# Expected durations of a hand-made instruction order reset, and its stream of weights rearranged

## The chip, the cores and the metric

The kernel runs on one core of a Trainium2 chip. The time is the device time of one execution in microseconds (us). A core has engines that run side by side, each taking its own queue of instructions strictly in order: TensorE (PE; PEld is its loading of weights), VectorE (DVE), ScalarE (ACT), GpSimd (POOL), and the queue of SyncE (SP), which here issues nearly all the transfers.

## The reference

One layer of a decoder trunk on 512 tokens of 1024 channels, in float32:

```
h = RMSNorm(x);  P = h @ W_in
y_A = attention: an indexer scores all keys, each query keeps its 128 best, softmax over those, 8 heads
y_B = HGRN2, a gated linear recurrence in chunks, 4 heads of 128, times silu(hg)
y_C = cb * causal_conv3(cc * ch)
x  += W_o( sum_b sigmoid(g_b) * (y_b @ U_b) )
x  += W_down relu(RMSNorm(x) @ W_up)^2
```

Columns of `W_in` are called kv (keys, values and the indexer's key), iq, aq (queries), hf, hq, hi, hg (HGRN2), cc, ch, cb (convolution) and g0, g1, g2 (the gates of attention, HGRN2 and convolution).

## The kernel before

**The stream.** All weights pass once, in 142 pieces ("slabs") of 128 rows times up to 1024 columns, in the order of `PLAN` (L32 to L47). For each slab SP loads `raw`, ACT rounds it to `whi` (fp32r), DVE forms `wlo = raw - whi` (L302 in `splitter`), and PE makes three products for each 128 x 128 block and 512 tokens (`whi` with the high and the low part of the other operand, `wlo` with the high part): 24 products of 512 columns for a full slab. Two `raw`, three `whi` and three `wlo` buffers stand between these steps. PE sums into tiles named `A` and the column's name (`Ahg`, `Ag`, `Au`, `Awo`, `Aup`, `Adn`).

**Beside the stream** run tasks. `index_task` chooses the best keys by 48 pairs of MAX and MATCH_REPLACE on DVE (L669, L670). `scan_task` takes each HGRN2 head through seven levels: an exponential on ACT (`Am`), a product on POOL (`Am` with `KQ`), two additions on DVE (`X`), products on PE (`pa`, or sums over channels `psum`, fed by a split `sh`, `sl`) and masked copies into `at` (L928, L945). `soft_task`, `soft_block`, `out_task` and `pv` do the attention of one head after another: logits (`pl`), softmax in `p`, transposes (`pt`), a split into `ph` and `pl`, products with the values (`po`), and `ya`; two heads make one of the four channel tiles of y_A. `pairs(b)` splits each finished channel tile of a branch into `yp`, which the raises `u` of that branch (`Au`) read. The raises of convolution (2), HGRN2 (1) and attention (0) follow in that order.

**What sets the order.** Class `Order` writes out the order of instructions of every engine when the program is built; the chip then only follows it. It keeps an expected clock for each engine. Every instruction has an expected duration `c` (L286 to L343), and a task's instruction is put on its engine's queue when what it reads is expected to be there. The stream goes first:

```
if e == "PE" and not main:
    at += self.SLACK                       # 250 ns
...
if not main and task.prio > 0 and e != "PE" and self.clk[e] > now + self.LIM:   # 900 ns
    self.push(self.clk[e] - self.LIM, task)
```

So a task's DVE, ACT or POOL work is put off while that engine is expected to be over 900 ns ahead of PE, and a task's product on PE is placed 250 ns after its operands are expected. The products of stream and tasks share PE's one queue: a task's product whose operand is late holds the stream behind it.

Of the kernel before, what the change touches and what calls it, by code (L numbers as in the profile page):

```python
# [21 lines left out]
EPS = 1e-6  # L22
# [9 lines left out]
def make_plan():  # L32
    plan = [("kv", 0)]
    plan += [("hf", j) for j in range(1, 4)] + [("hq", j) for j in range(4)] + [("hi", 0)]
    plan += [("hg", j) for j in range(4)] + [("aq", 0)]
    plan += [(c, j) for j in range(4) for c in ("cc", "ch", "cb")]
    for b in BRANCHES:
        for q in range(2):
            plan += [(f"g{b}", 4 * q + j) for j in range(4)] + [(f"u{b}", q)]
    plan += [("wo", j) for j in range(8)]  # L40
    for f in range(2):
        plan += [("up", 16 * f + j) for j in range(16)] + [("dn", 8 * f + j) for j in range(8)]
    return plan
# [6 lines left out]
def slabs_of(name, j):  # L50
    """The pieces of weights of one entry of the plan: matrix, first row, row blocks, first column, columns."""
    if name in FIRST_COL:
        return [("in", 0, 8, FIRST_COL[name] + 128 * j, 128)]
    if name == "kv":
        return [("kv", 0, 3, 0, 324), ("kv", 384, 3, 0, 324), ("kv", 768, 2, 0, 324)]
    if name in ("hi", "aq"):
        return [("in", 256 * i, 2, C_HI if name == "hi" else C_AQ, 512) for i in range(4)]
    if name[0] == "u" and name != "up":
        return [(name, 0, 4, 512 * j + 256 * i, 256) for i in range(2)]
    if name in ("wo", "up"):  # L60
        return [(name, 0, 8, 128 * j, 128)]
    return [("dn", 2048 * (j // 8) + 1024 * i, 8, 128 * (j % 8), 128) for i in range(2)]
# [34 lines left out]
class Order:  # L97
    """Fixes the order of instructions on each engine: the stream of weights runs through, and each of the tasks
    beside it goes on when what it reads is expected to be there."""

# [51 lines left out]
    def step(self, task, main=False):  # L152
        """Goes on with a task as far as it can now; for the main stream only one group of products at a time."""
        while True:
# [97 lines left out]
def kernel(ctx: ExitStack, tc: tile.TileContext, xT, x, wst, slabs, vecs, rel, ident_d, masks_d,  # L252
# [26 lines left out]

# [1 line left out]
    def in_psum(*aps):  # L281
# [4 lines left out]
    def act(out_, in_, func, scale=None, bias=None, accum=None):  # L286
        kw = {}
        c = 100 + 0.83 * size(in_)
        if scale is not None:
            kw["scale"] = scale  # L290
            c += 0 if isinstance(scale, float) else 93
        if bias is not None:
            kw["bias"] = bias
            c += 93
        if accum is not None:
            kw["accum_out"] = accum
            c += 90
        return Op("A", c, [in_, scale, bias], [out_, accum], lambda: A.activation(out_, in_, func, **kw))  # L298

    def tt(out_, a, b, op, e="V"):  # L300
        c = 65 + 1.06 * size(out_) if e == "V" else 110 + 2.2 * size(out_)
        return Op(e, c, [a, b], [out_], lambda: (V if e == "V" else G).tensor_tensor(out_, a, b, op))  # L302

    def ts(out_, a, s1, s2, op0, op1=None, e="V"):
        n = size(out_)
        c = (65 + (1.06 if in_psum(a) else 0.53) * n) if e == "V" else 100 + 1.0 * n
        eng = V if e == "V" else G
        f = (lambda: eng.tensor_scalar(out_, a, s1, s2, op0)) if op1 is None else (
            lambda: eng.tensor_scalar(out_, a, s1, s2, op0, op1))
        return Op(e, c, [a, s1, s2], [out_], f)  # L310

    def stt(out_, a, s, b, op0, op1):
        return Op("V", 65 + 1.06 * size(out_), [a, s, b], [out_],
                  lambda: V.scalar_tensor_tensor(out_, a, s, b, op0, op1))

    def red(out_, in_):
        return Op("V", 65 + 1.06 * size(in_), [in_], [out_], lambda: V.tensor_reduce(out_, in_, AX.X, ALU.add))

    def cp(out_, in_, e="V"):
        c = 65 + (1.06 if in_psum(in_) else 0.53) * size(out_) if e == "V" else 100 + 1.0 * size(out_)  # L320
        return Op(e, c, [in_], [out_], lambda: (V if e == "V" else G).tensor_copy(out_, in_))

    def recip(out_, in_):
        return Op("V", 60 + 6.3 * size(out_), [in_], [out_], lambda: V.reciprocal(out_, in_))

# [3 lines left out]
    def mm(ps, a, b, start, stop):  # L329
        n = size(b)  # L330
        if a.dtype == F32R:
            c = 0.4167 * n + (15 if n < 512 else 0) if n >= 192 else 213
        else:
            c = (218 if size(a) > 64 else 125) if n <= 128 else 1.68 * n
        return Op("PE", c, [a, b] + ([] if start else [ps]), [ps], lambda: PE.matmul(ps, a, b, start=start, stop=stop))  # L335
# [26 lines left out]

# [1 line left out]
    A.preload_act_table_set("natural_log_exp_and_others")  # L364
# [15 lines left out]
    def rsqrt(dst, a, tmp, n):  # L380
        """The inverse square root of a / n + EPS, by Newton's steps from the exponent; a becomes minus half of that."""
        yield ts(a, a, -0.5 / n, -0.5 * EPS, ALU.mult, ALU.add)
        yield ts(dst.bitcast(I32), a.bitcast(I32), -0.5, float(0x5F3759DF - (1 << 30) - (1 << 22)), ALU.mult, ALU.add)
        for _ in range(3):
            yield tt(tmp, dst, dst, ALU.mult)
            yield tt(tmp, tmp, a, ALU.mult)
            yield stt(dst, tmp, 1.5, dst, ALU.add, ALU.mult)

# [1 line left out]
    NSL = len(SLABS)  # L390
# [80 lines left out]

# [1 line left out]
    def stack(dst, ps, odd, scale=None):  # L473
# [141 lines left out]

# [1 line left out]
    def bias_task():  # L617
# [25 lines left out]
    def index_task(tb):  # L643
# [24 lines left out]
        for _ in range(16):  # L668
            yield [Op("V", 65 + 1.05 * n, [w], [mx], lambda: V.max(mx, w)),  # L669
                   Op("V", 65 + 1.05 * n, [w, mx], [w], lambda: V.match_replace(w, mx, w, GONE))]  # L670
        yield ts(w, w, -2e38, NEG, ALU.is_ge, ALU.mult)
# [95 lines left out]
    def soft_block(h, tb, pl, pb, cb, st, p):  # L767
        n = pb.shape[1]
        s = st[:, 4 * tb:4 * tb + 4]
        yield Op("V", 65 + 1.06 * n, [pl, cb], [p, st], lambda: V.tensor_tensor_reduce(  # L770
            pb, pl[:, :n], cb[:, OFF[tb]:OFF[tb] + n], -1.0, -GONE, ALU.add, ALU.min, s[:, 0:1]))
        free(pl)
        yield act(pb, pb, AF.Exp, scale=-1.0, bias=s[:, 0:1], accum=s[:, 2:3])
        yield recip(s[:, 3:4], s[:, 2:3])
        yield act(pb, pb, AF.Copy, scale=s[:, 3:4])
        put(("p", h, tb), (p, st))
        if tb == 3:
            free(cb)
# [46 lines left out]

# [1 line left out]
    def half(t, m):  # L827
# [51 lines left out]
    def over_channels(prod, n):  # L879
        """Sums over the partitions, on every partition."""  # L880
        hi_t = yield Get("w2", "sh", F32R)
# [18 lines left out]
    def near(h, lv, Am, at):  # L900
        """The first levels, where a block has few pairs: products of the pairs, then sums over the channels."""
        pr = yield Get("w2", "prd")
# [13 lines left out]
        if lv == 0:  # L916
            o3 = at.rearrange("p (c b i) -> p c b i", c=4, i=2)[:, :, :, 1]
            mk = masks[:, 0, None, 1::2].to_broadcast([128, 4, 64])
            d3 = pd[:, :256].rearrange("p (c b) -> p c b", c=4)
            yield Op("V", 65 + 1.06 * 256, [pd, masks], [at], lambda: V.copy_predicated(o3, mk, d3))  # L920
        else:
            for i in range(2):
                for j in range(2):
                    o3 = at.rearrange("p (c b i) -> p c b i", c=4, i=4)[:, :, :, 2 + j]
                    mk = masks[:, 1 + i, None, 2::4].to_broadcast([128, 4, 32])
                    d3 = pd.rearrange("p (i c b j) -> p i c b j", i=2, c=4, j=2)[:, i, :, :, j]
                    yield Op("V", 65 + 1.06 * 128, [pd, masks], [at],
                             lambda o3=o3, mk=mk, d3=d3: V.copy_predicated(o3, mk, d3))  # L928
# [3 lines left out]
    def level(h, lv, Am, at):  # L932
# [9 lines left out]
        if m < 32:  # L942
            mk = masks[:M, lv + 1, None, m:].to_broadcast([M, 4, M])
            yield Op("V", 65 + 1.06 * 4 * M, [pa, masks], [at],
                     lambda: V.copy_predicated(at3[:M, :, m:], mk, pa3[:M, :, m:]))  # L945
# [49 lines left out]

# [1 line left out]
    X1 = [None] * 8  # L997
# [74 lines left out]

# [1 line left out]
    def cols(n, m0, name, ev, rhs):  # L1074
        """Out channels on partitions, all tokens in one product."""
        h, l, h3, l3 = yield Need(("w", n))
# [13 lines left out]
    def rows(n0, cnt, name, ev, lhs, ncol):  # L1090
        """Tokens on partitions."""
        pss = {}
# [29 lines left out]
    def start():  # L1122
        """The first three channel tiles together, as their weights and the tokens arrive."""
        ps = []
# [157 lines left out]
```

## Time and profile before

| | |
|---|---|
| median of 3 runs | 904.72 us (904.61 to 906.04) |
| span of the profiled execution, first to last instruction | 903.0 us |
| around the span, taken against the median | 1.7 us |
| PE busy | 869.9 us, 96% |
| DVE busy | 565.6 us, 63% |
| ACT, POOL busy | 353.6 us, 39%; 149.8 us, 17% |
| mean granted TensorE clock | 0.995 |

The page gives no time of the profiled execution other than its span, so the 1.7 us is the distance of the span from the median. Shares of busy time are means over stages that differ: the first third of the span holds the tasks, the rest almost only the stream. A product's listed time is longer than its distance from the next one, since products overlap, so a short wait of PE can hide in its busy time.

### The profile page before, as it was taken

To read this page: it belongs to the slowest core of one execution; us is meant where nothing else is said; L and a number is where in the kernel's file an instruction comes from. 1 tells how busy PE (TensorE), PEld (TensorE's weight loads), DVE (VectorE), ACT (ScalarE), POOL (GpSimd) and SP (SyncE) were. 2 spreads that over 40 slices of the span, in tenths; PEclk is the share of its full clock that TensorE was granted. 3 is DMA by queue.
4 is the path that set the end of the run, shared out by engine and by line. 5 is a ranking of instruction groups with operands and counts; after the bars stand their busy time and mean duration, and the time that the engine had idled before them with its cause. 6 is when DMAs were issued, how large, how long until landed. Compare 5 with 4: busy or idle time off the path is not lost.

```text
span 903.0 us, 10635 instructions
## 1 busy us (share of the span) xinstructions
PE 869.9 (96%) x4060; PEld 720.0 (80%) x4060; DVE 565.6 (63%) x972; ACT 353.6 (39%) x562; POOL 149.8 (17%) x129
## 2 busy tenths in 40 slices
PE   7999999887898999999999999999999999999997
PEld 6888877765677888888888888888888888888886
DVE  5589999999999766665654645444443344444331
ACT  6662434322364546556333333333311133342110
POOL 0010124346473111150200031000011100000000
PEclk9999999999999999999999999999999999999999
DMA  8434222122112212211222522222322222223330
GB/s 299 157 136 147 94 70 73 68 71 71 47 46 71 70 71 71 94 70 71 93 94 94 187 95 92 94 94 101 109 94 94 97 90 95 105 104 105 127 118 24
DMA packets 27611, 88.08 MB, mean 98 GB/s; under 512 B 2928, under 2 KB 5800, under 8 KB 27560
## 3 DMA queue, kind: packets, MB, share of 16 engines
q1 hardware_dynamic: 27528, 87.38, 27.6%
q8 instruction: 32, 0.52, 0.2%
q14 instruction: 19, 0.16, 0.0%
q0 software_dynamic: 32, 0.02, 0.0%
HBM read 85.28 MB, written 3.68 MB: 99 GB/s over the span
## 4 chain that ended last, share of the span: by engine, by line
PE 72%; DVE 25%; issue 2%; DMA 0%; POOL 0%; ACT 0%; DVEq 0%; POOLq 0%
PE Aup L335 19%; PE Adn L335 19%; PE Ag L335 12%; PE Au L335 7%; PE Awo L335 5%; DVE wlo L302 4%; DVE wk L670 3%; DVE mx L669 3%; DVE X L302 2%; PE Ast L335 2%; PE Akv L335 1%; PE Ahf L335 1%; PE po L335 1%; PE pl L335 1%; DVE at L928 1%
## 5 line engine op out<-in xcount | busy, mean ns | idle before, releaser
L298 ACT ACTIVATE whi<-raw 128x1024 fp32r<-128x1024 f32 (+2 forms) x150 | 153.8, 1026 | 252.9 <-PE Adn L335 124.5
L302 DVE TENSOR_TENSOR wlo<-raw,whi 128x1024 fp32r<-128x1024 f32 (+2 forms) x150 | 192.2, 1281 | 59.0 <-ACT whi L298 58.5
L335 PE MATMUL Aup<-x2h,whi 128*128 128x512 f32 x256 | 100.0, 391 | 0.0
L335 PE MATMUL Aup<-x2h,wlo 128*128 128x512 f32 x256 | 99.6, 389 | 0.0
L335 PE MATMUL Aup<-x2l,whi 128*128 128x512 f32 x256 | 99.6, 389 | 0.0
L335 PE MATMUL Adn<-hl,whi 128*128 128x512 f32 x256 | 99.6, 389 | 0.0
L335 PE MATMUL Adn<-hh,wlo 128*128 128x512 f32 x256 | 99.6, 389 | 0.0
L335 PE MATMUL Adn<-hh,whi 128*128 128x512 f32 x256 | 99.6, 389 | 0.0
L302 DVE TENSOR_TENSOR rl<-rl 128x512 f32<-128x512 f32 x32 | 22.2, 692 | 96.4 <-ACT hh L298 96.4
L335 PE MATMUL Ag<-xhi,whi 128*128 128x512 f32 x192 | 76.6, 399 | 0.0
L335 PE MATMUL Ag<-xhi,wlo 128*128 128x512 f32 x192 | 75.2, 392 | 0.0
L335 PE MATMUL Ag<-xlo,whi 128*128 128x512 f32 x192 | 75.0, 391 | 0.0
L298 ACT ACTIVATE rl<-Aup 128x512 f32<-128x512 f32 x32 | 19.1, 598 | 110.2 <-PE Aup L335 110.2
L335 PE MATMUL Au<-yp,whi 128*128 128x512 f32 x192 | 60.6, 396 | 0.0
L302 POOL TENSOR_TENSOR Am<-Am,KQ 128x512 f32<-128x512 f32 x28 | 42.1, 1504 | 95.1 <-ACT Am L298 95.1
L335 PEld LDWEIGHTS Aup<-x2l,whi 128*128 128x128 f32 x256 | 48.1, 188 | 10.3 <-issue 0.2
L335 PEld LDWEIGHTS Aup<-x2h,whi 128*128 128x128 f32 x256 | 48.1, 188 | 10.2 <-issue 0.2
L335 PEld LDWEIGHTS Adn<-hh,whi 128*128 128x128 f32 x256 | 48.1, 188 | 10.1
L335 PEld LDWEIGHTS Adn<-hl,whi 128*128 128x128 f32 x256 | 48.0, 188 | 10.0
L335 PEld LDWEIGHTS Aup<-x2h,wlo 128*128 128x128 f32 x256 | 48.0, 188 | 9.9
L335 PEld LDWEIGHTS Adn<-hh,wlo 128*128 128x128 f32 x256 | 48.0, 188 | 9.9
L298 ACT ACTIVATE p<-p,st 128x128 f32<-128x128 f32 (+3 forms) x64 | 35.0, 556 | 25.1 <-DVE st L770 20.5
(261 smaller groups left out, 1713.1 us busy)
## 6 DMA issues: line engine op xcount, KB each, us to landing
raw<-in_slabs_dram SPq DMA_DIRECT2D x139, 512.0 KB, 3.2
xt<-in_x_dram SPq DMA_DIRECT2D x8, 256.0 KB, 5.8
x<-in_xT_dram SPq DMA_DIRECT2D x4, 512.0 KB, 5.6
out_dram<-o SPq DMA_DIRECT2D x7, 256.0 KB, 2.0
xin<-in_xT_dram SPq DMA_DIRECT2D x3, 512.0 KB, 5.8
d<-d SPq DMA_DIRECT2D x1, 1536.0 KB
raw<-in_wst_dram SPq DMA_DIRECT2D x3, 384.0 KB, 5.5
toep<-d SPq DMA_DIRECT2D x1, 1024.0 KB, 5.5
```

What stands on the lines that cost most here:

```text
L298: return Op("A", c, [in_, scale, bias], [out_, accum], lambda: A.activation(out_, in_, func, **kw))
L302: return Op(e, c, [a, b], [out_], lambda: (V if e == "V" else G).tensor_tensor(out_, a, b, op))
L335: return Op("PE", c, [a, b] + ([] if start else [ps]), [ps], lambda: PE.matmul(ps, a, b, start=start, stop=stop))
L669: yield [Op("V", 65 + 1.05 * n, [w], [mx], lambda: V.max(mx, w)), Op("V", 65 + 1.05 * n, [w, mx], [w], lambda: V.match_replace(w, mx, w, G ...
L670: Op("V", 65 + 1.05 * n, [w, mx], [w], lambda: V.match_replace(w, mx, w, GONE))]
L928: lambda o3=o3, mk=mk, d3=d3: V.copy_predicated(o3, mk, d3))
```

## The change

Three things: the expected durations `c` are set to other values; in the plan, aq and the convolution's columns come ahead of hg; and all eight gate tiles of a branch come ahead of its two raises. No instruction is added or taken away, and nothing else in `Order` is changed.

```diff
-    plan += [("hf", j) for j in range(1, 4)] + [("hq", j) for j in range(4)] + [("hi", 0)]
-    plan += [("hg", j) for j in range(4)] + [("aq", 0)]
-    plan += [(c, j) for j in range(4) for c in ("cc", "ch", "cb")]
+    plan += [("hf", j) for j in range(1, 4)] + [("hq", j) for j in range(4)] + [("hi", 0), ("aq", 0)]
+    plan += [(c, j) for j in range(4) for c in ("cc", "ch", "cb")] + [("hg", j) for j in range(4)]
     for b in BRANCHES:
-        for q in range(2):
-            plan += [(f"g{b}", 4 * q + j) for j in range(4)] + [(f"u{b}", q)]
+        plan += [(f"g{b}", j) for j in range(8)] + [(f"u{b}", q) for q in range(2)]
...
     def act(out_, in_, func, scale=None, bias=None, accum=None):
-        c = 100 + 0.83 * size(in_)
+        c = 190 + 0.83 * size(in_)
...
     def tt(out_, a, b, op, e="V"):
-        c = 65 + 1.06 * size(out_) if e == "V" else 110 + 2.2 * size(out_)
+        c = 145 + 1.05 * size(out_) if e == "V" else 185 + 2.2 * size(out_)
...
     def stt(out_, a, s, b, op0, op1):
-        return Op("V", 65 + 1.06 * size(out_), [a, s, b], [out_],
+        return Op("V", (145 if isinstance(s, float) else 205) + 1.05 * size(out_), [a, s, b], [out_],
...
     def mm(ps, a, b, start, stop):
-            c = 0.4167 * n + (15 if n < 512 else 0) if n >= 192 else 213
+            c = 0.4167 * n + 13.5 if n >= 192 else 213
...
-            yield [Op("V", 65 + 1.05 * n, [w], [mx], lambda: V.max(mx, w)),
-                   Op("V", 65 + 1.05 * n, [w, mx], [w], lambda: V.match_replace(w, mx, w, GONE))]
+            yield [Op("V", 145 + 1.05 * n, [w], [mx], lambda: V.max(mx, w)),
+                   Op("V", 235 + 1.05 * n, [w, mx], [w], lambda: V.match_replace(w, mx, w, GONE))]
...
-            yield Op("V", 65 + 1.06 * 256, [pd, masks], [at], lambda: V.copy_predicated(o3, mk, d3))
+            yield Op("V", 720, [pd, masks], [at], lambda: V.copy_predicated(o3, mk, d3))
...
-                    yield Op("V", 65 + 1.06 * 128, [pd, masks], [at],
+                    yield Op("V", 930, [pd, masks], [at],
```

The other helpers on DVE (`ts`, `red`, `cp`, `recip`, the masked copy of L945, the softmax's subtraction of L770) get 80 to 170 ns more in the same way. Lines after L47 move up by one or two in the changed kernel.

What this does to the order is seen at two places. The first is DVE's queue in the convolution's columns, before. A row is an instruction; `wlo` is a slab's split, `os` and `qt`, `qr` small steps of inverse square roots, `yc`, `cb`, `u`, `zc` the convolution's, `mx` and `wk` the choice of keys.

```order
L302 TENSOR_TENSOR wlo_1819<-raw_1730,whi_1817 128x1024
L321 COPY stt_1829<-pss_1830 128x128
L314 SCALAR_TENSOR_TENSOR stt_1829<-stt_1829,dec_1729,pss_1830 128x128 x2
L302 TENSOR_TENSOR qt<-qr 128x32
L314 SCALAR_TENSOR_TENSOR os_1540<-os_1540 128x4
L302 TENSOR_TENSOR sl_1832<-prd_1789,sh_1791 128x512
L314 SCALAR_TENSOR_TENSOR yc_1841<-u_1815,vec,yc_1841 128x511
L302 TENSOR_TENSOR sl_1867<-prd_1827,sh_1851 128x256
L302 TENSOR_TENSOR X_1770<-X_1770 128x128x2 x2
L314 SCALAR_TENSOR_TENSOR yc_1841<-u_1815,vec,yc_1841 128x510
L302 TENSOR_TENSOR cb_1906<-Acb_1811,R 128x512
```

Two more instructions stand behind these before the next split. The same queue after the change, from one split of the convolution's columns to the next:

```order
L300 TENSOR_TENSOR wlo_1717<-raw_1650,whi_1715 128x1024
L668 MAX mx_674<-wk_508 128x8
L669 MATCH_REPLACE wk_508<-mx_674,wk_508 128x384
L313 SCALAR_TENSOR_TENSOR yc_1733<-u_1713,vec,yc_1733 128x511
L300 TENSOR_TENSOR cb_1762<-Acb_1709,R 128x512
L300 TENSOR_TENSOR os_1516<-os_1516 128x4
L668 MAX mx_693<-wk_510 128x8
L669 MATCH_REPLACE wk_510<-mx_693,wk_510 128x512
L300 TENSOR_TENSOR wlo_1766<-raw_1701,whi_1764 128x1024
```

Fewer task instructions stand between two splits. Counted over the twenty splits from the 14th of 128 x 1024 to the 34th, DVE's queue holds 281 instructions before and 210 after.

The second place is PE's queue where attention's last head ends, before. `pt` are transposes of the softmax, `po` products with the values, `Au` the raise of HGRN2.

```order
L335 MATMUL po_3809<-pl_3852,vst 128x384
L335 MATMUL Au_728_3874<-yp_3188,whi_3747 128x512 x2
L335 MATMUL Au_728_3874<-yp_3188,wlo_3749 128x512
L340 MATMUL pt_3884<-ident,p_3666 128x128
L335 MATMUL Au_728_3874<-yp_3202,whi_3747 128x512 x2
L335 MATMUL Au_728_3874<-yp_3202,wlo_3749 128x512
L335 MATMUL Au_728_3874<-yp_3218,whi_3747 128x512 x2
L335 MATMUL Au_728_3874<-yp_3218,wlo_3749 128x512
L335 MATMUL po_3809<-ph_3866,vst 128x256
L335 MATMUL po_3809<-pl_3867,vst 128x256
```

The head's steps lie among products of the stream, and four gate tiles of attention follow before its first raise. After the change, PE reaches the first raise of attention (`Au_769`) while the last head is still to come:

```order
L334 MATMUL Au_769_4191<-yp_3741,whi_4076 128x512 x2
L334 MATMUL Au_769_4191<-yp_3741,wlo_4078 128x512
L334 MATMUL Au_769_4191<-yp_4064,whi_4076 128x512 x2
L334 MATMUL Au_769_4191<-yp_4064,wlo_4078 128x512
L339 MATMUL pt_4216<-ident,p_4037 128x128 x4
L339 MATMUL pt_4228<-ident,p_4037 128x128 x3
L334 MATMUL po_4215<-ph_4224,vst 128x512
L334 MATMUL po_4215<-pl_4225,vst 128x512
L339 MATMUL pt_4238<-ident,p_4037 128x128 x2
L339 MATMUL pt_4245<-ident,p_4037 128x128
```

Six more `po` products follow, and then the raise goes on with the fourth channel tile, which the last head completes:

```order
L334 MATMUL po_4215<-ph_4241,vst 128x256
L334 MATMUL po_4215<-pl_4242,vst 128x256
L334 MATMUL po_4215<-ph_4247,vst 128x192
L334 MATMUL po_4215<-pl_4248,vst 128x192
L334 MATMUL Au_769_4191<-yp_4262,whi_4076 128x512 x2
L334 MATMUL Au_769_4191<-yp_4262,wlo_4078 128x512
```

From the first `pt` of that head to its last `po` no product of the stream stands in the queue.

## Rows read from the trace of the kernel before

**Rows 1.** The page's part 1: engine, busy us, share, instructions.

```profile
PE 869.9 (96%) x4060; PEld 720.0 (80%) x4060; DVE 565.6 (63%) x972; ACT 353.6 (39%) x562; POOL 149.8 (17%) x129
```

**Rows 2.** Stretches: length, busy us (instructions) by engine, granted clock, DMA share, GB/s.

```profile
50.00:75.00 25.00, 25.00 (x115) 20.07 (x114) 23.70 (x45) 15.38 (x25) 4.62 (x5) 1.00 0.48 169
...
125.00:300.00 175.00, 152.98 (x771) 122.85 (x770) 171.69 (x325) 68.92 (x111) 83.57 (x64) 0.98 0.18 64
300.00:440.00 140.00, 140.00 (x703) 116.84 (x702) 89.11 (x216) 78.13 (x158) 27.06 (x31) 1.00 0.21 73
```

**Rows 3.** Waits of PE, 100 to 300 us: who waited, for whom, us, times, longest.

```profile
PE pa L335 <- POOL Am L302: 5.1, 4, 2.3
PE psum L335 <- DVE sl L302: 2.6, 2, 1.5
PE pq L340 <- DVE os L302: 2.3, 1, 2.3
```

**Rows 4.** Timeline of PE around one wait: start us, us, instruction, idle before.

```profile
188.23 0.39 PE L335 MATMUL Ach<-xhi,wlo 128*128 128x512 f32 x1
190.48 0.97 PE L335 MATMUL pa<-Am 128*64 128x64 f32 x8 [1.86 <-POOL Am L302]
191.39 0.80 PE L335 MATMUL Ach<-xhi,whi 128*128 128x512 f32 x1
191.98 0.63 PE L335 MATMUL Ach<-xlo,whi 128*128 128x512 f32 x1
192.41 0.63 PE L335 MATMUL Ach<-xhi,wlo 128*128 128x512 f32 x1
```

**Rows 5.** Stretches of 1 us around that wait, columns as in rows 2.

```profile
191.00:192.00 1.00, 1.00 (x7) 0.79 (x6) 0.94 (x5) 0.74 (x1) 0.00 (x0) 0.50 0.84 320
193.00:194.00 1.00, 1.00 (x4) 0.81 (x3) 1.00 (x2) 0.26 (x1) 1.00 (x1) 0.50 0.00 0
194.00:195.00 1.00, 1.00 (x5) 0.77 (x5) 1.00 (x1) 0.00 (x0) 1.00 (x2) 0.96 0.00 0
```

**Rows 6.** Timeline of DVE: the 14th and the 34th split of 128x1024.

```profile
106.77 2.14 DVE L302 TENSOR_TENSOR wlo<-raw,whi 128x1024 fp32r<-128x1024 f32 x1
...
275.40 1.99 DVE L302 TENSOR_TENSOR wlo<-raw,whi 128x1024 fp32r<-128x1024 f32 x1
```

**Rows 7.** DVE's groups by shape: out<-in, count, busy us, mean ns, idle before.

```profile
L302 DVE TENSOR_TENSOR wlo<-raw,whi 128x1024 fp32r<-128x1024 f32 x139 | 184.6, 1328 | 57.4 <-ACT whi L298 57.0
L302 DVE TENSOR_TENSOR X<-X 128x256 f32<-128x256 f32 x56 | 32.1, 573 | 1.0
L670 DVE MATCH_REPLACE8 wk<-mx,wk 128x512 f32<-128x512 f32 x16 | 10.8, 676 | 0.0
L314 DVE SCALAR_TENSOR_TENSOR hz<-hth,hz 128x512 f32<-128x512 f32 x4 | 4.2, 1058 | 0.0
```

**Rows 8.** Timeline of POOL beside the split at 106.77 us.

```profile
107.91 1.48 POOL L302 TENSOR_TENSOR prd<-Am 128x256 f32<-128x256 f32 x1
```

**Rows 9.** Timeline of PE, ACT and DVE: the last head of attention.

```profile
422.92 0.60 PE L340 MATMUL pt<-ident,p 128*128 128x128 f32 x4
423.55 0.60 ACT L298 ACTIVATE ph<-pt 128x512 fp32r<-128x512 f32 x1
424.18 0.69 DVE L302 TENSOR_TENSOR pl<-pt,ph 128x512 fp32r<-128x512 f32 x1
430.89 0.28 DVE L302 TENSOR_TENSOR pl<-pt,ph 128x128 fp32r<-128x128 f32 x1
433.78 0.59 ACT L298 ACTIVATE yb<-po 64x512 f32<-64x512 f32 x1 [3.04 <-PE po L335]
435.91 0.69 DVE L302 TENSOR_TENSOR ya<-po,yb 64x512 f32<-64x512 f32 x1
```

**Rows 10.** The chain that ended last: start us, us, what.

```profile
462.37 10.88 PE Au L335 x48
505.89 43.52 PE Awo L335 x192
```

More of the change, by code (lines that the diff above doesn't have):

```diff
@@ L296, in act @@
             kw["accum_out"] = accum
[L297 removed]
+            c += 190
         return Op("A", c, [in_, scale, bias], [out_, accum], lambda: A.activation(out_, in_, func, **kw))
     def tt(out_, a, b, op, e="V"):
[L301 removed]
+        c = 145 + 1.05 * size(out_) if e == "V" else 185 + 2.2 * size(out_)
         return Op(e, c, [a, b], [out_], lambda: (V if e == "V" else G).tensor_tensor(out_, a, b, op))
@@ L305, in ts @@
         n = size(out_)
-        c = (65 + (1.06 if in_psum(a) else 0.53) * n) if e == "V" else 100 + 1.0 * n
+        c = (145 + (1.05 if in_psum(a) else 0.53) * n) if e == "V" else 100 + 1.0 * n
+        c += 60 if e == "V" and not isinstance(s1, float) else 0
         eng = V if e == "V" else G
@@ L312, in stt @@
     def stt(out_, a, s, b, op0, op1):
-        return Op("V", 65 + 1.06 * size(out_), [a, s, b], [out_],
+        return Op("V", (145 if isinstance(s, float) else 205) + 1.05 * size(out_), [a, s, b], [out_],
                   lambda: V.scalar_tensor_tensor(out_, a, s, b, op0, op1))
     def red(out_, in_):
-        return Op("V", 65 + 1.06 * size(in_), [in_], [out_], lambda: V.tensor_reduce(out_, in_, AX.X, ALU.add))
+        return Op("V", 145 + 1.05 * size(in_), [in_], [out_], lambda: V.tensor_reduce(out_, in_, AX.X, ALU.add))
     def cp(out_, in_, e="V"):
-        c = 65 + (1.06 if in_psum(in_) else 0.53) * size(out_) if e == "V" else 100 + 1.0 * size(out_)
+        c = 145 + (1.05 if in_psum(in_) else 0.53) * size(out_) if e == "V" else 100 + 1.0 * size(out_)
         return Op(e, c, [in_], [out_], lambda: (V if e == "V" else G).tensor_copy(out_, in_))
     def recip(out_, in_):
-        return Op("V", 60 + 6.3 * size(out_), [in_], [out_], lambda: V.reciprocal(out_, in_))
+        return Op("V", 140 + 6.3 * size(out_), [in_], [out_], lambda: V.reciprocal(out_, in_))
     def mset(out_, v, e="V"):
@@ L769, in soft_block @@
         s = st[:, 4 * tb:4 * tb + 4]
-        yield Op("V", 65 + 1.06 * n, [pl, cb], [p, st], lambda: V.tensor_tensor_reduce(
+        yield Op("V", 235 + 1.05 * n, [pl, cb], [p, st], lambda: V.tensor_tensor_reduce(
             pb, pl[:, :n], cb[:, OFF[tb]:OFF[tb] + n], -1.0, -GONE, ALU.add, ALU.min, s[:, 0:1]))
@@ L943, in level @@
             mk = masks[:M, lv + 1, None, m:].to_broadcast([M, 4, M])
-            yield Op("V", 65 + 1.06 * 4 * M, [pa, masks], [at],
+            yield Op("V", 200 + 1.05 * 4 * M, [pa, masks], [at],
                      lambda: V.copy_predicated(at3[:M, :, m:], mk, pa3[:M, :, m:]))
```

## The prediction

> **What bounds the kernel now.** I read the page's busy times first, then PE by stretches, then whom PE waits for, then single waits in the timeline. Over the span PE is busy 96% and DVE 63% [rows 1], which would make PE the bound throughout. The stretches say otherwise. From 50 us on DVE is nearly full, 23.70 of 25.00 us, while PE still has no idle time; from 125 to 300 us DVE is busy 171.69 of 175.00 us and PE only 152.98; from 300 us on PE has no idle time again and DVE 89.11 of 140.00 [rows 2]. In the stage from 125 to 300 us both engines are close to full and PE is the one that waits: for POOL's `Am`, for DVE's splits `sl` and small steps `os`, each wait up to 2.3 us [rows 3]. None of these is the stream's own split. What waits is a product of a task, and since PE takes its queue in order the stream stands behind it.
>
> How much is lost there? The idle time is 175.00 - 152.98 = 22.0 us. More hides in the busy time, since a product of 512 columns is listed at 0.39 us while undisturbed products start 0.227 us apart (192 in 43.52 us, [rows 10]). Taking every product of 125 to 300 us (771, [rows 2]) from its start to the next start, less the smallest usual distance of its shape, gives 34.4 us in all. I use 34.4, of which 22.0 is certain. The same sum over 300 to 440 us (703 products) gives 4.5 us, and over the rest almost nothing but the start.
>
> A check by another way. DVE's 14th wide split starts at 106.77 us and its 34th at 275.40 [rows 6]: 168.6 us. In that time PE's queue holds 20 slabs, 481 products of the stream at 0.227 us, 109.0 us, and 155 task products at 0.18 us (eight records of `pa` take 0.97 us, of which the last one's tail is some 0.25 [rows 4]), 27.9 us: 136.9 us of work in 168.6 us, 31.7 us lost. DVE's queue holds 281 instructions there, 0.60 us each. DVE sets the pace of this stage.
>
> **The change part by part.**
>
> *Expected durations.* Nothing that an engine executes gets shorter. What moves is how much task work is put between two splits. A split was expected at 65 + 1.06 x 1024 = 1150 ns and takes 1328 on average; one of the additions on `X` at 336 and takes 573; a MATCH_REPLACE of 512 at 603 and takes 676, with its load of values besides [rows 7]. The clock on which tasks are released ran fast, so DVE's queue got more work per slab than PE's work covers. After the change the expectations are 1220, 414 and 773 ns: on the whole no longer too short, though `X` still is, and the last step of `hz` too (743 against 1058, [rows 7]). Over the same twenty splits DVE's queue now holds 210 instructions. Taking each kind that is left out from start to next start, the 71 fewer ones (10 on `X`, 6 pairs of MAX and MATCH_REPLACE, 4 masked copies, 10 of the steps `os`, 8 of the softmax and its operands and others) are worth 31 us of the 158.6 us that the 281 come to by the same measure. That leaves 127.5 us; the real stretch was 168.6 / 158.6 = 1.063 times the sum, so 135.5 us. PE's work there is the same 481 products and 114 task products, 109.0 + 20.5 = 129.5 us. DVE is then 6.0 us short instead of 31.7. Outside of these twenty splits 34.4 - 31.7 = 2.7 us stay. The loss of the stage goes from 34.4 to 8.7 us: 25.7 us gained. Bounds: at the plain mean of 0.60 us the 210 instructions take 126 us, less than PE, and only the 2.7 us stay; at the other end half of 34.4 stays, 17 us, if single waits for POOL and for small steps go on as in [rows 3], since a task product is still placed only 250 ns after its operand is expected. I take 8.7, next to the sum by rows.
>
> *Where the 31 us go.* The same instructions now stand later. From 300 to 440 us DVE has 140.00 - 89.11 = 50.9 us free [rows 2], which covers them. If it didn't, the stream's splits would be late there; three buffers of splits stand in front of PE.
>
> *Queries and convolution ahead of hg.* The four `hg` tiles carry two DVE instructions and one of ACT each, the costlier 1.06 us [rows 7], and are wanted only when a head's output is ready. They move behind the convolution, and the queries' steps move up; loads on SP's queue follow the stream's order with the same size and spacing, and the DMA share is 0.18 [rows 2]. I cost it at nothing beyond the count above; it could be worth 4 x 1.7 = 7 us either way if DVE's excess were spread otherwise, which lies inside the bounds of the first part.
>
> *Eight gate tiles ahead of the raises.* Product for product PE's work is the same. For HGRN2 and the convolution the raise comes later, so its input has more time. For attention the order shows the opposite: the queue reaches the first raise while the last head is still to be transposed, and from there to the head's last `po` no product of the stream follows. Before, `ya` of the last head ended at 435.91 + 0.69 = 436.6 us and its raise began at 462.37 [rows 9, 10]: 25.8 us of cover that are gone. The new wait, from the rows of that head: `pt` 0.60, `ph` 0.60, four `pl` of 0.69, about 0.55 and 0.42 (between the sizes shown) and 0.28, the last `po` about 0.3, `yb` 0.59, `ya` 0.69, and a split `yp` like `ph` and `pl` again, 0.60 + 0.69: 6.0 us, and 0.3 us for nine handovers of 0.03 us (`pt` ends at 423.52, `ph` starts at 423.55). PE has 10 transposes and 8 products of its own in that time, 2.0 us. It waits 4.3 us.
>
> A wait has an aftermath: after the 1.86 us wait at 188.6 us [rows 4] the granted clock is 0.50, the lower of the two levels (1.2 GHz), until 194 us [rows 5], and products start 0.43 us apart instead of 0.227, about eight of them, 1.6 us. Not each wait of 2 us brings this, since the mean clock of the stage is 0.98 [rows 2]; a longer one probably, not surely, does. I price the new wait at 4.3 + 1.6 = 5.9, rounded to 6 us. Bounds: 4 without the clock; 13 if the head takes as long as it took before, 436.6 - 422.92 = 13.7 us with `yp` 1.3 more and PE's 2.0 less [rows 9]. The Trainium skill, "TensorE: Matmul & The Clock Gate", Part 1, says that the throttled state is the default and activity releases it, so an idle array falls back to half speed. By that rule the 1.6 us are to be counted here in any case, and without it the wait would be 4.3 us; the trace agrees at 188 us.
>
> *The sum.* The span of 903.0 us and the 1.7 us around it are the median of 904.72. 904.7 - 25.7 + 6.0 = 885.0 us.
>
> **The rivals.**
>
> A. PE runs almost dense. The 210 instructions fit under PE's work and only 2.7 us of the stage's loss stay, with the short wait of 4 at the raise: 904.7 - 31.7 + 4 = 877 us. For it: 126 us at the mean price against 129.5 of PE. Against: PE waits for single late operands even where DVE has time, 4.5 us of loss from 300 to 440 us.
>
> B. Half of the waits stay. `Am` is the largest releaser [rows 3], and POOL's expected times are still short where its access is strided (748 ns for `prd`, which takes 1.48, [rows 8]). 17 us stay and the wait at the raise is 13: 904.7 - 17.2 + 13 = 900 us. Against: DVE, not POOL, was full.
>
> C. Slower, by VectorE and GpSimd in each other's way. The split at 106.77 us took 2.14 us with POOL's products running beside it, against 1.33 on average [rows 6 to 8]. If every split of the forty slabs from 100 to 320 us fell beside a POOL product, DVE would need 40 x 0.81 = 32 us more in a stretch where it has none to spare, and the raise would wait 13: 904.7 - 25.7 + 32 + 13 = 924 us. It turns slower at 25.7 - 6 = 20 us, that is 25 of the 40 splits. For it: the new expectations describe an engine that is not disturbed, and DVE is kept full to 900 ns. Against: POOL's work is the same, and the mean of 1328 ns holds such cases already. The Trainium skill, "SBUF — State Buffer", Who interferes with whom, has a rule for this: the two engines share one pair of ports as an exclusive lock, and the loser blocks for the whole instruction. The trace agrees with the 2.14 us; the rule doesn't say how often they meet.
>
> D. The reset changes no wait that matters: both effects cancel, 904 us. The count of 281 against 210 speaks against it.
>
> **How the numbers follow.** My forecast has 0.60, A 0.19, B 0.13, C 0.05, D 0.03. Its own range is 880 to 892 us. The range for 8 in 10 takes in A and most of B's way: 874 to 899 us; A with another 3 us of the later stage's loss gone is the low end. About 0.2% (1.8 us) is what a measurement can tell from no change: faster by more has 0.60 + 0.19 + 0.13 = 0.92, less a little of B, 0.91; within it 0.04; slower 0.05.
>
> **What would show it.** In the changed profile PE's idle time from 125 to 300 us should fall from 22 us to under 7, with DVE still at nine tenths and DVE staying busy longer, past 300 us. A wait of PE of 3 to 6 us in total should stand at the first raise of attention, for ACT or DVE of the last head (`ph`, `pl`, `yp`), with the granted clock below 1 for some us after it. From the `Awo` products to the end the two traces should have the same length, 903.0 - 505.9 = 397.1 us [rows 10]. The prediction is wrong if the waits of 1 to 2 us for `Am`, `sl` and `os` are as many as before, if splits take clearly over 1.33 us on average, or if the wait at the raise is over 10 us.

## The result, and the profile after

The changed kernel takes 888.29 us (median of 4 runs, 887.41 to 890.11) beside 905.07 us (4 runs, one more than ahead of the prediction) of the kernel before on the same chip: a ratio of 0.9813, with a 95% interval of 0.98 to 0.9825. The forecast was 885.0 us and faster, with a range of 874 to 899. The profiled execution took 887.85 us, its span is 886.1 us against 903.0 before.

The page's busy times and its chain of waits, after:

```profile
PE 866.7 (98%) x4060; PEld 719.7 (81%) x4060; DVE 564.5 (64%) x972; ACT 353.8 (40%) x562; POOL 151.4 (17%) x129
...
PE 92%; DVE 6%; ACT 1%; DMA 0%; issue 0%; ACTq 0%; POOLq 0%
```

The work of each engine is the same as in [rows 1]; only its order differs. Of the chain that ended last 92% is now PE's, 72% before. Stretches after (length, busy us and instructions of PE, PEld, DVE, ACT, POOL, granted clock, DMA share, GB/s):

```profile
125.00:300.00 175.00, 171.35 (x860) 141.59 (x859) 167.46 (x300) 70.70 (x98) 75.38 (x55) 1.00 0.24 79
300.00:440.00 140.00, 139.99 (x709) 116.82 (x707) 103.53 (x239) 77.73 (x155) 38.24 (x41) 1.00 0.23 76
```

Beside [rows 2], PE's idle time from 125 to 300 us is 3.65 us instead of 22.0. DVE has 300 instructions there instead of 325, and 14.4 us more work from 300 to 440 us. PE's waits over the whole span (us, times, longest):

```profile
PE Ast L334 <- ACT xhi L296: 6.3, 1, 6.3
PE psum L334 <- DVE sl L300: 2.7, 2, 1.5
PE Au L334 <- ACT yp L296: 2.1, 1, 2.1
PE Akv L334 <- DVE iqs L300: 1.7, 1, 1.7
```

The first is the start, as before. Of the three of [rows 3], those for `Am` and `os` are gone and that for `sl` stands as it was. New is a wait of 2.1 us for `yp` in a raise.

Where did the time go? In what follows "loss" is the measure of the prediction: from each product of PE to the start of the next, less the undisturbed distance of its shape, summed over a stretch.

| loss, us | 0 to 125 | 125 to 300 | 300 to 440 | 440 to 500 | all |
|---|---|---|---|---|---|
| before | 5.4 | 34.9 | 5.0 | 0.0 | 45.7 |
| after | 6.6 | 8.8 | 5.1 | 7.6 | 28.5 |

The sums, which take in 0.4 us behind 500 us, differ by 17.2 us, the spans by 16.9. The level hangs on which distance counts as undisturbed: the prediction had 34.4 us for the stage before, and with the median distance of each shape it is 36.3 before and 9.8 after. The differences hardly move by that, and the argument rests on them.

**The stage from 125 to 300 us.** DVE's 14th and 34th wide split, in its timeline after:

```profile
107.27 1.22 DVE L300 TENSOR_TENSOR wlo<-raw,whi 128x1024 fp32r<-128x1024 f32 x1 [1.08 <-ACT whi L296]
...
244.30 1.22 DVE L300 TENSOR_TENSOR wlo<-raw,whi 128x1024 fp32r<-128x1024 f32 x1
```

They are 137.0 us apart where [rows 6] had 168.6. DVE's groups by shape, after:

```profile
L300 DVE TENSOR_TENSOR wlo<-raw,whi 128x1024 fp32r<-128x1024 f32 x139 | 192.0, 1381 | 58.9 <-ACT whi L296 58.4
L300 DVE TENSOR_TENSOR X<-X 128x256 f32<-128x256 f32 x56 | 30.0, 536 | 1.0
```

Against [rows 7] a split became 53 ns longer on average and an addition on `X` 37 ns shorter: no slowdown of DVE as a whole.

**The raise of attention.** PE, ACT and DVE there, after (start us, us, instruction, idle before and for whom):

```profile
461.71 0.50 PE L334 MATMUL po<-ph,vst 128*128 128x512 f32 x1 [0.36 <-ACT ph L296]
...
464.42 0.32 PE L334 MATMUL po<-pl,vst 128*128 128x192 f32 x1
464.78 0.59 ACT L296 ACTIVATE yb<-po 64x512 f32<-64x512 f32 x1 [1.03 <-PE po L334]
465.41 0.68 DVE L300 TENSOR_TENSOR ya<-po,yb 64x512 f32<-64x512 f32 x1 [1.08 <-ACT yb L296]
466.12 0.63 ACT L296 ACTIVATE yp<-ya 128x512 fp32r<-128x512 f32 x1 [0.75 <-DVE ya L300]
466.80 0.51 PE L334 MATMUL Au<-yp,whi 128*128 128x512 f32 x1 [2.06 <-ACT yp L296]
```

From the last `po` to the first product on the new `yp` three short steps follow one another (`yb`, `ya`, `yp`), with nothing for PE beside them. `ya` ends at 465.41 + 0.68 = 466.1 us. In [rows 9] that tile was done by 436.6 us, long before the raise at 462.37. The stretches of 2 us around it, columns as above:

```profile
464.00:466.00 2.00, 0.67 (x4) 0.48 (x3) 0.92 (x5) 0.59 (x1) 0.00 (x0) 1.00 0.05 8
466.00:468.00 2.00, 0.98 (x3) 0.61 (x4) 0.78 (x2) 0.63 (x1) 0.00 (x0) 1.00 0.00 0
468.00:470.00 2.00, 2.00 (x8) 1.57 (x7) 1.38 (x2) 0.00 (x0) 0.00 (x0) 0.71 0.00 0
470.00:472.00 2.00, 2.00 (x6) 1.57 (x5) 0.00 (x0) 0.00 (x0) 0.00 (x0) 0.50 0.00 0
472.00:474.00 2.00, 2.00 (x9) 1.61 (x9) 1.33 (x3) 1.58 (x2) 0.00 (x0) 0.94 0.00 0
```

The granted clock falls to its lower level only two microseconds after the wait. Eight products from 468.79 to 472.17 us take 3.38 us instead of 8 x 0.227 = 1.8. So 1.6 of the 7.6 us are clock and 6.0 are waits.

**The start and the end.** DVE's queue at the start, after:

```profile
22.71 1.01 DVE L300 TENSOR_TENSOR iqs<-Ast,iqs 64x384 fp32r<-64x384 f32 x2 [0.69 <-ACT iqs L296]
23.75 0.83 DVE L300 TENSOR_TENSOR wlo<-raw,whi 128x648 fp32r<-128x648 f32 x1
24.84 1.03 DVE L300 TENSOR_TENSOR iqs<-Ast,iqs 64x384 fp32r<-64x384 f32 x2 [0.25 <-ACT iqs L296]
```

and the same place before:

```profile
21.70 2.14 DVE L302 TENSOR_TENSOR iqs<-Ast,iqs 64x384 fp32r<-64x384 f32 x4 [1.08 <-ACT iqs L298]
24.03 0.83 DVE L302 TENSOR_TENSOR wlo<-raw,whi 128x648 fp32r<-128x648 f32 x1 [0.19 <-ACT whi L298]
```

The new expectations put a split between the four `iqs`, and PE, which wants the last one, waits 1.7 us where it waited 0.7. At the other end the chain's last part is the one of [rows 10]; 886.1 - 488.93 = 397.2 us against 397.1:

```profile
488.93 43.52 PE Awo L334 x192
```

### The profile page after: what moved, and what is told of

It is laid out like the page before. It is cut to its first block, busy times and chain, and to the rows that moved or that the text cites. A ratio compares the mean times of both kernels' runs of the same rounds, so it can differ in the third digit from the quotient of the medians.

```text
span 886.1 us, 10647 instructions
## 1 busy us (share of the span) xinstructions
PE 866.7 (98%) x4060; PEld 719.7 (81%) x4060; DVE 564.5 (64%) x972; ACT 353.8 (40%) x562; POOL 151.4 (17%) x129
## 4 chain that ended last, share of the span: by engine, by line
PE 92%; DVE 6%; ACT 1%; DMA 0%; issue 0%; ACTq 0%; POOLq 0%
PE Aup L334 20%; PE Adn L334 20%; PE Ag L334 15%; PE Au L334 7%; PE Awo L334 5%; PE Aaq L334 2%; PE Ahq L334 2%; PE Ahi L334 2%; PE Ahf L334 2%; PE Ahg L334 2%; PE Ast L334 2%; PE pa L334 2%; PE Ach L334 2%; PE Akv L334 2%; PE Acc L334 1%; PE pl L334 1%
## 5 line engine op out<-in xcount | busy, mean ns | idle before, releaser
L300 DVE TENSOR_TENSOR wlo<-raw,whi 128x1024 fp32r<-128x1024 f32 (+2 forms) x150 | 199.5, 1331 | 60.6 <-ACT whi L296 59.9
L334 PEld LDWEIGHTS Au<-yp,whi 128*128 128x128 f32 x192 | 35.8, 192 | 9.6 <-ACT yp L296 2.2
```

## The experiments

Each ran beside the kernel before, which had medians of 905.36 to 905.62 us in them. Losses in us over the four stretches of the table above. Lines left out of an edit are marked by `...`.

| kernel | us | ratio, 95% | losses |
|---|---|---|---|
| the change | 888.29 | 0.9813 [0.98, 0.9825] | 6.6, 8.8, 5.1, 7.6 |
| 1 durations only | 908.36 | 1.0032 [1.0019, 1.0044] | 6.4, 24.8, 7.5, 8.2 |
| 2 gates as before | 895.46 | 0.9889 [0.9875, 0.9902] | 6.8, 9.0, 9.5, 10.4 |
| 3 columns as before | 893.47 | 0.9864 [0.9849, 0.9879] | 6.9, 9.8, 10.7, 7.3 |
| 4 late tile last | 887.58 | 0.9803 [0.979, 0.9817] | 6.5, 8.9, 4.6, 7.7 |
| 5 gates only | 905.23 | 0.9996 [0.9987, 1.0005] | 5.8, 34.8, 4.9, 0.0 |
| 6 durations, 7 wide buffers | 901.05 | 0.9956 [0.9944, 0.9969] | 6.3, 11.5, 8.9, 13.7 |
| 7 attention first | 883.12 | 0.9756 [0.9743, 0.977] | 6.9, 7.7, 4.7, 3.5 |
| 8 DVE expected x 0.9 | 897.97 | 0.9927 [0.9913, 0.994] | 8.2, 23.7, 4.9, 0.6 |
| 9 DVE expected x 1.1 | 902.85 | 0.9968 [0.9955, 0.998] | 6.7, 4.4, 15.7, 15.6 |
| 10 new for DVE and PE only | 884.35 | 0.9767 [0.9753, 0.978] | 6.4, 3.4, 7.8, 7.9 |
| 11 the change, 7 wide buffers | 888.28 | 0.9805 [0.9791, 0.9818] | 7.1, 9.4, 4.4, 7.4 |
| 12 7 and 4 together | 881.53 | 0.9733 [0.9719, 0.9746] | 6.7, 7.7, 4.7, 2.6 |

**1. The new durations with the old plan.** The changed kernel with these lines of before:

```diff
-    plan += [("hf", j) for j in range(1, 4)] + [("hq", j) for j in range(4)] + [("hi", 0), ("aq", 0)]
-    plan += [(c, j) for j in range(4) for c in ("cc", "ch", "cb")] + [("hg", j) for j in range(4)]
+    plan += [("hf", j) for j in range(1, 4)] + [("hq", j) for j in range(4)] + [("hi", 0)]
+    plan += [("hg", j) for j in range(4)] + [("aq", 0)]
+    plan += [(c, j) for j in range(4) for c in ("cc", "ch", "cb")]
...
-        plan += [(f"g{b}", j) for j in range(8)] + [(f"u{b}", q) for q in range(2)]
+        for q in range(2):
+            plan += [(f"g{b}", 4 * q + j) for j in range(4)] + [(f"u{b}", q)]
```

> The new expected durations with the old plan (hg ahead of aq, gate tiles four by four). Theory 1 (the durations bring the gain in the stage of 125 to 300 us, and delay attention; the order of gates and columns is worth little by itself): PE's loss from 125 to 300 us falls from 35 to about 9 us as in the changed kernel, and the wait at attention's first raise stands here as well, 5 to 10 us, because the durations brought it: 886 to 893 us. Theory 2 (as the prediction put it: the wait at the raise belongs to the eight gate tiles ahead of it): the loss falls the same, but no wait at the raise: about 881 us. Theory 3 (the gain comes from the order of columns): close to 905 us.

908.36 us, slower than before, which none of the three theories foresaw: Theory 3 comes near the number, but not by its mechanism. In the columns from aq to cb, where the old order lost 29.7 us, this one loses 1.6; but the products of the raises (`Au`, with the tasks among them) now lose 27.4 and the gate tiles 11.4. Its timeline at the convolution's first raise, POOL, PE and ACT:

```profile
238.08 1.73 POOL L302 TENSOR_TENSOR yc<-yc,cb 128x512 f32<-128x512 f32 x1
...
263.18 0.40 PE L336 MATMUL Au<-yp,wlo 128*128 128x512 f32 x1
...
278.65 2.35 POOL L302 TENSOR_TENSOR KQ<-KQ,X 128x1024 f32<-128x1024 f32 x1 [1.56 <-issue]
...
281.32 0.63 ACT L298 ACTIVATE yp<-yc 128x512 fp32r<-128x512 f32 x1 [2.80 <-DVE dec L322]
```

The convolution's last tile is ready at 239.8 us, and its split `yp` stands on ACT's queue only at 281.32. PE runs out of raise products at 263.6 us and then has only small task products, one wait after the other. Two of its stretches:

```profile
125.00:300.00 175.00, 161.90 (x785) 134.34 (x784) 163.73 (x301) 65.64 (x98) 74.04 (x55) 0.94 0.21 70
...
230.00:290.00 60.00, 47.16 (x223) 39.16 (x222) 54.17 (x106) 20.90 (x34) 25.25 (x21) 0.83 0.15 51
```

In the written order the split needs a buffer of 1024 columns, of which six exist. The convolution's first three `yp` hold three (their splits stand at 231.68 to 234.15 us), the scan's `KQ` and `X` the others, by the program; the split follows 0.3 us behind the last use of `X`, which ends at 281.00 us. So in the columns the durations do what they were priced at, and the old plan gives all of it back.

**2 and 3. One part of the plan set back.** In 2 the loop of the gates, in 3 the order of the columns is that of before.

```diff
-        plan += [(f"g{b}", j) for j in range(8)] + [(f"u{b}", q) for q in range(2)]
+        for q in range(2):
+            plan += [(f"g{b}", 4 * q + j) for j in range(4)] + [(f"u{b}", q)]
```

> The changed kernel with the gate tiles four by four again. Theory 1: the stream comes to attention's first raise four gate tiles (21.8 us) sooner while attention ends when it did, so PE waits there up to 20 us more, part of which the planner moves: 893 to 905 us. Theory 2 (the eight gate tiles bring the wait): no wait at the raise, about 881 us.

> The changed kernel with hg ahead of aq and the convolution again. Theory 1 (columns worth little): within 4 us of 888. Theory 3 (columns bring a large part): over 895 us. If the order of columns costs, under 884 us.

895.46 us, within Theory 1, and 893.47 us, between Theories 1 and 3. The loss of the stage is 9.0 and 9.8 us: it falls with either part of the old plan too. Each part is worth something with the new durations: by the ratios (0.9889 and 0.9864 against 0.9813, of 905 us) the gates 6.9 us and the columns 4.6, both together (1.0032) 19.8. Either alone undoes most of what held up experiment 1. And the gates ahead of the raises don't make the wait at attention's raise: without them the loss there is larger, 10.4 us against 7.6.

**4. The late tile last.** In attention's first raise, four output tiles take three channel tiles first, and the one that the last head completes at the end.

```diff
...
+        for ks in ((0, 1, 2), (3,)):
+            for i in range(4):
...
+                for k in ks:
+                    yield Need(rhs[0](k))
...
```

> The changed kernel, where attention's first raise makes its first four output tiles together in four accumulators: all products of the first three channel tiles of y_A first (36 products, 8.2 us), then those of the fourth, which the last head completes. Nothing is left out. If the wait at the raise with its stretch of half clock costs the 7.1 us that the sum of distances gives, this takes most of it back: 881 to 883 us, no stretch of lower clock after it. If the time there is only moved (the raise's evacuations are then late for the output projection): 886 to 888 us.

887.58 us, with 0.7 us less by the medians: the intervals overlap, and the time is only moved, the second of the two expectations. PE's timeline:

```profile
467.61 0.36 PE L334 MATMUL po<-pl,vst 128*128 128x192 f32 x1
470.03 0.58 PE L334 MATMUL Au<-yp,whi 128*128 128x512 f32 x1 [2.07 <-ACT yp L296]
```

The products ahead of the wait are more, but the head's own products are placed among them: its last `po` starts at 467.61 us instead of 464.42, and the three steps behind it still have nothing beside them. A further 1.6 us is lost where `Awo` waits for `ml`.

**5. The gates alone.** The kernel before with the new line for the gates. The order of the columns alone, and both plan changes together, were not run with the old durations: when the order is written out with them, the stream comes to wait for good.

> The old durations and columns, only the eight gate tiles of a branch ahead of its raises. Theory (the gain of the stage from 125 to 300 us comes from the durations; the plan's order only gives them room): PE's loss there stays near 35 us and nothing else changes, 902 to 908 us. Rival (the plan's order brings a part of the gain by itself): under 898 us.

905.23 us, no change. Its stretches:

```profile
125.00:300.00 175.00, 155.32 (x770) 125.33 (x769) 171.46 (x324) 68.40 (x110) 83.61 (x64) 0.96 0.19 64
...
440.00:500.00 60.00, 60.00 (x266) 49.66 (x265) 30.89 (x38) 20.83 (x28) 2.17 (x3) 1.00 0.30 99
```

The stage's loss is that of before, and at attention's raise, with all eight gate tiles ahead of it, PE has no idle time.

**6. Durations, the old plan, and a seventh wide buffer.** This tests the cause named under 1.

```diff
-("w2", sp, (128, 512), 39), ("w4", sp, (128, 1024), 6)
+("w2", sp, (128, 512), 37), ("w4", sp, (128, 1024), 7)
```

> The new expected durations with the old plan, as in the first experiment (908.4 us), but with 7 buffers of 128 x 1024 instead of 6 (and 37 of 128 x 512 instead of 39). Theory: with the new durations the HGRN2 tasks run later and still hold four of the six wide buffers (KQ) and one for the scan when the stream comes to the convolution's raise, whose four split inputs yp need four; the wait of PE from 262 to 280 us there is a wait for a buffer. Then a seventh buffer takes away some 15 to 20 us: 888 to 895 us, with the waits at the raises of HGRN2 and attention still there. Rival (the convolution's own steps on POOL and DVE are late, not a buffer): within 3 us of 908.

901.05 us: faster than 1 by 7 us, and slower than expected. Its stretches:

```profile
230.00:290.00 60.00, 55.70 (x273) 45.73 (x272) 56.52 (x100) 23.85 (x34) 25.45 (x21) 0.97 0.23 76
...
440.00:500.00 60.00, 54.86 (x224) 42.65 (x223) 32.93 (x56) 24.64 (x44) 0.00 (x0) 0.91 0.19 63
```

The hole at the convolution's raise is closed, PE's idle time from 230 to 290 us falling from 12.8 to 4.3 us, and the stage's loss falls by 13.3. But 5.5 us more are lost at attention's raise and 1.4 from 300 to 440 us. The cause is confirmed, the price was not: a stream that comes sooner meets tasks that are no further.

**7. Attention's tasks first.** The changed kernel, with attention's tasks at the stream's own priority (those of the softmax and of the products with the values, too) and the seventh buffer.

```diff
...
-    spawn(q_task())
+    spawn(q_task(), 0)
-    spawn(soft_task())
-    spawn(out_task())
+    spawn(soft_task(), 0)
+    spawn(out_task(), 0)
...
```

> The changed kernel with the seventh wide buffer and the tasks of attention at the stream's priority (0 instead of 1). If the last head ends sooner so that part of the wait at attention's first raise (7.1 us with its slow stretch) goes: 883 to 887 us. If the head's pace is set by its own chain of steps and not by the place it gets: within 1.5 us of 888.

883.12 us, 5 us less than the change; the loss at the raise is 3.5 us instead of 7.6. PE's wait, and the stretches around it:

```profile
462.71 0.50 PE L334 MATMUL Au<-yp,whi 128*128 128x512 f32 x1 [2.06 <-ACT yp L296]
...
460.00:462.00 2.00, 0.65 (x5) 0.43 (x4) 0.83 (x2) 0.59 (x1) 0.00 (x0) 1.00 0.50 137
462.00:464.00 2.00, 1.07 (x4) 0.67 (x4) 0.69 (x1) 0.63 (x1) 0.00 (x0) 1.00 0.33 133
464.00:466.00 2.00, 2.00 (x10) 1.69 (x9) 1.38 (x2) 0.00 (x0) 0.00 (x0) 1.00 0.00 0
```

The last wait for `yp` is still there, 2.06 us; the short ones in the head before it are gone, and this time the clock stays up.

**8 and 9. DVE's expectations scaled.** One line where an instruction is written into the order:

```diff
+        if op.e == "V":
+            op.c *= 0.9      # 1.1 in the other
```

> The changed kernel with the expected durations of VectorE taken at nine tenths. Theory (two opposite costs hang on this number: too short, and PE waits for late operands in the stage; too long, and the tasks come late to the raises): the loss from 125 to 300 us rises from 9 to 15 to 22 us, the wait at attention's raise (7 us) goes: 888 to 897 us. Rival (the loss of the stage does not depend on them, since single waits for POOL and small steps make it): 880 to 883 us.

> The changed kernel with the expected durations of VectorE taken at eleven tenths; at nine tenths it took 898.0 us with a loss of 23.7 us from 125 to 300 us and 0.6 us after 440. Theory (two opposite costs): the loss of the stage falls under 6 us, the waits at the raises of HGRN2 and attention grow to 20 us or more: 896 to 910 us. Rival (the loss that is left in the stage, 8.8 us, comes of expectations still too short, and the tasks have room): 880 to 886 us.

897.97 and 902.85 us, both slower than the 888.29 between them, for opposite reasons. The first lies a little above what was expected (897 us, and 23.7 us of loss against 22). At 0.9:

```profile
125.00:300.00 175.00, 162.13 (x811) 131.79 (x810) 171.62 (x312) 68.47 (x100) 84.63 (x63) 0.98 0.21 70
...
440.00:500.00 60.00, 60.00 (x272) 49.63 (x272) 34.76 (x49) 22.88 (x33) 0.00 (x0) 1.00 0.30 97
```

and at 1.1:

```profile
125.00:300.00 175.00, 174.28 (x870) 144.94 (x869) 158.43 (x279) 70.02 (x96) 69.31 (x48) 1.00 0.25 82
300.00:440.00 140.00, 133.86 (x649) 110.48 (x648) 108.03 (x243) 66.05 (x128) 41.55 (x41) 0.95 0.22 72
440.00:500.00 60.00, 53.10 (x239) 41.40 (x238) 39.45 (x91) 35.05 (x76) 6.25 (x9) 0.94 0.16 53
```

With shorter expectations DVE gets 312 instructions in the stage and PE waits 12.9 us there, but not at the raise. With longer ones DVE gets 279, PE waits 0.7 us in the stage and then 6.1 and 6.9 us behind it.

**10. New expectations for DVE and PE only.** ACT's and POOL's stay as before.

```diff
-        c = 190 + 0.83 * size(in_)
+        c = 100 + 0.83 * size(in_)
...
-            c += 190
+            c += 90
...
-        c = 145 + 1.05 * size(out_) if e == "V" else 185 + 2.2 * size(out_)
+        c = 145 + 1.05 * size(out_) if e == "V" else 110 + 2.2 * size(out_)
```

> The changed kernel with the old expected durations of ScalarE and GpSimd; VectorE's and TensorE's stay new. Theory (VectorE is the full engine, so its expectations decide): within 4 us of 888, the loss from 125 to 300 us at most 13 us. Rival (the waits for POOL's Am and ACT's steps need theirs too): the loss is 16 us or more, 895 us or above.

884.35 us, 4 us less than with all of them. The gain doesn't need the values for ACT and POOL, which cost some of it. In the stage the loss is 3.4 us instead of 8.8, and the waits for `sl` are gone from its list; why is open. PE's own new values (13.5 ns more for a product of 512 columns) are in every run with new durations; what they do alone was not tried.

**11. The buffer without the priorities.** The change with the edit of 6.

> The changed kernel with only the seventh wide buffer, without attention's priority (both together took 883.1 us). If the priority of attention brings the gain: 886 to 889 us, with the wait of some 7 us at attention's raise. If the buffer does: 883 to 884 us.

888.28 us: the seventh buffer is worth nothing here by itself, so the gain of 7 comes from the priorities. Whether they need the buffer is not shown; they were not run without it.

**12. Edits 7 and 4 together.**

> Attention's priority and the seventh buffer together with the first raise of attention that takes its fourth channel tile last. Alone the latter gave 0.7 us, since the last head's steps stood behind the products put ahead of them. With the head ahead by its priority, the products of the first three tiles should cover the rest of its chain: the 3.5 us lost after 440 us go to under 1, 880 to 881 us. If the chain is stretched again: within 1 us of 883.

881.53 us (880.11 to 882.07), the best of all. No wait for `yp` is left in its list of waits. The loss at the raise is 2.6 us, not under 1 as expected: PE still waits 1.6 us where `Awo` wants `ml`. With a head that isn't behind, keeping the late tile for the end seems to bring something, 1.6 us by the medians, but the two intervals overlap, from 0.9743 to 0.9746.

## Why the prediction was right, and where it was not

**The expected durations.** The step held, nearly to its number. Twenty splits were to take 135.5 us and took 137.0, PE's work there being 129.5 by the same sum. The loss of the stage was to go from 34.4 to 8.7; it went from 34.9 to 8.8. PE's idle time is under the 7 us named, and DVE is at 96% there and busier past 300 us. Experiments 5, 8 and 9 tie it to the expectations: without them the loss stays at 34.8, at 0.9 of DVE's it is 23.7, at 1.1 it is 4.4. The plan doesn't bring this gain, since with either part of it set back the loss is 9.0 and 9.8 (experiments 2 and 3); it keeps the gain from being lost elsewhere, as in experiment 1. Of the signs named, one came in part: a split takes 1.38 us on average, a little over 1.33.

**Where the 31 us go.** The step "from 300 to 440 us DVE has 50.9 us free, which covers them" is true of DVE's time and was the wrong question. What comes later is not only a load on DVE but a head, a `yp`, a buffer that a raise waits for. With the old plan that gave back everything, 908.36 us (experiment 1).

**The columns, costed at nothing.** This step failed. With the new durations the order of the columns is worth 4.6 us (experiment 3), inside the bound of 7 but not nothing. With the old columns PE waits 4.2 us for `oq` at 239 us, in experiments 1, 3 and 6 alike; after the change this wait is gone. But that is not where the 4.6 us lie: the stage as a whole loses 9.8 us in experiment 3 and 8.8 after the change. From 300 to 440 us it loses 10.7 against 5.1, where PE waits for attention's logits `pl` and the granted clock is at its lower level for some us from 307.7 us on. From the waits of experiment 3:

```profile
PE py L340 <- DVE oq L301: 4.2, 1, 4.2
...
PE pl L335 <- DVE at L301: 2.0, 1, 2.0
```

So what the prediction had at nothing is not DVE's excess spread otherwise, but tasks that come late further on.

**The wait at attention's raise.** Its place, its chain and nearly its size were right: priced at 4.3 us of waits and 1.6 of clock, it is 6.0 and 1.6. Its cause was wrong. "25.8 us of cover that are gone" was put down to the eight gate tiles ahead of the raise. They alone make no wait (experiment 5, 0.0), and setting them back makes it longer (experiment 2, 10.4). The later tasks used up the cover, the last head's `ya` ending at 466.1 us instead of 436.6: the shorter DVE's expectations, the smaller this loss, 15.6, 7.6 and 0.6 us at 1.1, 1.0 and 0.9. So the part of the change that was booked as the cost is worth 6.9 us to it. The forecast had nearly the right sum with one term under the wrong name. That term's size was no luck, since it was read from the order after the change; that it was subtracted for the gate tiles was a mistake that the total alone would not have shown.

**The start.** 1.2 us more are lost in the first 125 us, most of it at `iqs`, of which the prediction said nothing. The sum: 25.7 - 6.0 = 19.7 us of gain were expected; 26.1 - 7.6 - 1.2 - 0.1 = 17.2 are measured by the losses, 16.8 by the medians. Of the 2.5 us between the two sums the raise has 1.6 and the start 1.2.

**The rivals.** A (dense, 877) did not come: 8.8 us of the stage's loss stay, not 2.7, and the raise costs 7.6, not 4. Neither did B (half the waits stay, 900): those for `Am` and `os` are gone. Its reading of [rows 8] was wrong besides. The 1.48 us of that `prd` are not its own length, expected at 748 ns, which was about right: seven of the twelve such products before take 0.61 to 0.80 us, and this one ends 0.5 us behind the split. Nor did it hold up the split at 106.77 us, which had begun before it; the product of POOL ahead of it did:

```profile
106.31 1.53 POOL L302 TENSOR_TENSOR Am<-Am,KQ 128x512 f32<-128x512 f32 x1 [32.70 <-ACT Am L298]
```

C (VectorE and GpSimd in each other's way, 924) is seen in single splits; one of 2.85 us and the product of POOL beside it, after:

```profile
200.08 2.40 POOL L300 TENSOR_TENSOR KQ<-KQ,X 128x1024 f32<-128x1024 f32 x1 [2.32 <-ACT X L296]
200.71 2.85 DVE L300 TENSOR_TENSOR wlo<-raw,whi 128x1024 fp32r<-128x1024 f32 x1
```

But over all 139 splits it is 7.4 us more (192.0 against 184.6), and PE's loss in that stage is what was forecast. D (no change) was wrong. It describes experiment 5, in which the durations are left alone.

## What to carry to other kernels

Where a program lays out its instructions by expected durations, a wrong duration moves work in time rather than making it slow: too short crowds the busiest engine early, too long delivers results late, and here a tenth either way on DVE cost 10 to 15 us. Nor is the true value always the best: with ACT's and POOL's left too short the kernel was 4 us faster. Setting the estimates right is half the change; the other half is to ask of everything that now comes later who reads it, which buffers it holds until then, and whether the order leaves room ahead of that reader. And a new wait is not put down to the edit that is nearest to it in the program without a run of that edit alone.

## What the runs showed of the hardware

Three waits of PE for the same `yp` were equally long, 2.06, 2.07 and 2.06 us (the change, experiments 4 and 7), and had different aftermaths: the clock fell in the first two (to 0.50, and to 0.58 and 0.57 over two stretches of 2 us) and stayed at 1.00 in the third, though in 4 and in 7 PE was at work without a gap until shortly before it. What decides is not shown. The Trainium skill, "TensorE: Matmul & The Clock Gate", Part 1, calls the throttled state the default, which activity releases. The prediction took from it that the 1.6 us come with such a wait in any case, which the page doesn't say; the third wait shows that an idle time of this length need not bring it.

The split at 200.71 us ends 1.08 us after POOL's product (200.08 + 2.40 = 202.48 us), as if it had waited for POOL and then run; an undisturbed one takes 1.22 us. It is no single case. In the traces before and after, 51 splits of 128 x 1024 start while a product of POOL runs, and 47 of them end 1.08 to 1.09 us behind that product. The other way round the split keeps its time and POOL waits, after:

```profile
154.45 1.21 DVE L300 TENSOR_TENSOR wlo<-raw,whi 128x1024 fp32r<-128x1024 f32 x1
154.60 2.18 POOL L300 TENSOR_TENSOR yc<-yc,cb 128x512 f32<-128x512 f32 x1 [1.29 <-DVE yc L313]
```

The same product takes 1.29 us at 174.63 us, where it starts ahead of the split; here it ends 1.1 us behind the split. This agrees with the rule of the Trainium skill, "SBUF — State Buffer", SBUF: two separate sides, that an instruction of VectorE with two inputs in SBUF and one of GpSimd that reads SBUF exclude each other: whichever starts first has the shared ports for its whole length, and the other blocks.
